# Low parts of half the mixer's weights on GpSimd instead of VectorE

## The chip, the cores and the metric

The kernel runs on one core of a Trainium2 chip. The core has five engines that work side by side, each on its own queue in order: TensorE (PE) multiplies matrices into an accumulator memory (PSUM), VectorE (DVE), ScalarE (ACT) and GpSimd (POOL) work elementwise, SyncE (SP) issues the transfers from the large memory (HBM) into the fast one (SBUF). Semaphores tell one engine that another is done. The metric is the device time of one execution in microseconds, here the median of several runs.

## What is computed

Two layers (`DEPTH`) over 256 tokens of width 1024, each a gated feed-forward, a mixer, a cross attention and a second gated feed-forward, each followed by a normalisation of the sum with the input. The change lies in the mixer:

```python
z = h @ w_in[l]
cb, cc, ch, rq, rf, ri, rg, pu = jnp.split(z, split_at, axis=-1)
y_conv = short_gated_conv(ch, cb, cc, conv_w[l])
y_rec = hgrn2(rq, rf, ri, rg, lbs[l], rec_norm_g[l])
y_pool = multiscale_pool(pu, pool_w[l], pool_scale[l])
mix = jnp.concatenate([y_conv, y_rec, y_pool], axis=-1) @ w_out[l]
h = layer_norm(ALPHA * h + mix, ln_g[l, 1], ln_b[l, 1])
```

`hgrn2` is a gated linear recurrence in chunks of 64 tokens, four heads of 128; the short convolution has three taps; the pool takes sliding means over 2, 4, 8 and 16 tokens. All inputs are float32 and the result has to keep nearly that precision.

## The kernel before

**Two parts for each weight.** TensorE's fast float format keeps fewer bits than float32. So each weight is used as a sum of a high part (the weight rounded to that format) and a low part (what the rounding left), and the activations likewise; a product is high by high, high by low and low by high. `split` (line 58) makes both parts: ScalarE casts the high part (line 59), VectorE subtracts it from the source (line 60). In profiles the weight's parts are `whi` and `wlo`, the loaded weight is `raw`.

**Loading.** `load` (line 62) brings a block of rows and columns of a weight matrix. It takes 128 x 2048 elements at a time into one of three `raw` buffers, with one transfer on SyncE's queue, and splits each in two halves of 128 x 1024 (`s` is 0 or 1, line 77), each with a `whi` and a `wlo` tile of its own from rings of eight. A load of 512 columns over all 1024 rows is two `raw` buffers, so four halves; one of 256 columns is one buffer and two halves; a slab of the output matrix (256 rows, 1024 columns) is also one buffer and two halves. A `whi` or `wlo` tile is written again when TensorE has read its last use, a `raw` buffer when both halves have been cast and subtracted.

**The mixer's order in the program** (function `mixer`, line 518). `columns` (line 522) loads some columns of `w_in` and multiplies: the forget gate f (columns 1280), the query q (768); then v (1792, by its own loop); then the recurrence; the pool's input (2816, 256 columns); the convolution's first two thirds (0) and its last (512, 256 columns); the output gate (2304). `fill` then computes the second half of the attention's keys (`keys(l, 1)`, line 494), and `project_back` multiplies with four slabs of `w_out`.

**The recurrence** is a chain between TensorE and VectorE: two products with the identity (line 576), one product of q with f over 1024 elements (line 579), then seven levels, each with a copy of keys into `kc` (line 585), matmuls (line 591), two products that scale q and k (lines 607 and 608) and two masked copies of the matmuls' results into `AT` (line 610). Two powers on GpSimd (line 640) normalise the result.

**What sets the order.** Each engine runs its instructions in a fixed order, which a planner sets when the program is built, from its own estimates of durations; the program's text gives precedence but not the order itself. So TensorE's matmuls for the pool and the convolution stand interleaved with those of the recurrence. No order is written out by hand around the change. Before it, GpSimd has in the mixer only the powers and some small fills.

Of the kernel before, what the change touches and what calls it, by code (L numbers as in the profile page):

```python
# [8 lines left out]
F32 = mybir.dt.float32  # L9
# [3 lines left out]
ALU = mybir.AluOpType  # L13
# [7 lines left out]
DM = 1024  # L21
DFF = 2816
NT = SEQ // P
NK = DM // P
# [4 lines left out]
CHUNK = 512  # L29
# [17 lines left out]
def model(ctx: ExitStack, tc: tile.TileContext, t: dict, out: bass.AP):  # L47
    nc = tc.nc
# [6 lines left out]
        return ps.tile(list(shape), F32, tag=tag, name=tag)  # L55


    def split(hi, lo, src):
        nc.scalar.copy(hi, src)  # L59
        nc.vector.tensor_tensor(lo, src, hi.bitcast(F32), op=ALU.subtract)  # L60

    def load(src, k0, nk, c0, ncol, fine=False):


        hi, lo, todo = [], [], []
        step = 2048 // ncol
        for a in range(k0, k0 + nk, step):
            raw = wp.tile([P, 2048], F32, tag="raw", name="raw", bufs=3)
            raw = raw.rearrange("p (k c) -> p k c", c=ncol)
            half = step // 2  # L70
            part = 1 if fine else step
            for b in range(0, step, part):
                nc.sync.dma_start(
                    raw[:, b : b + part, :],
                    src[(a + b) * P : (a + b + part) * P, c0 : c0 + ncol].rearrange("(k p) c -> p k c", p=P),
                )
            for s in range(2):
                h = wp.tile([P, 1024], F32R, tag="whi", name="whi", bufs=8)
                w = wp.tile([P, 1024], F32R, tag="wlo", name="wlo", bufs=8)
                h = h.rearrange("p (k c) -> p k c", c=ncol)  # L80
                w = w.rearrange("p (k c) -> p k c", c=ncol)
                r = raw[:, s * half : (s + 1) * half, :]
                if fine:
                    todo += [(h[:, b, :], w[:, b, :], r[:, b, :]) for b in range(half)]
                else:
                    split(h, w, r)
                hi.append(h)
                lo.append(w)
        return Weights(hi, lo, half, todo)
# [20 lines left out]
    def mm_cols(w, cols, x):  # L110
        o = acc()
        for k in range(NK - 1):
            product(o, w.at(k, cols)[0], x[:, k], k == 0, False)
        for k in range(NK):
            product(o[:, 0, :], w.at(k, cols)[1], x[:, k, 0, :], False, False)
        product(o, w.at(NK - 1, cols)[0], x[:, NK - 1], False, True)
        return sums(o)

    def add(dst, o):
        dst = dst if len(dst.shape) == 3 else halves(dst)  # L120
        nc.scalar.copy(dst, o[:, 1])  # L121
        nc.vector.tensor_tensor(dst, o[:, 0], dst, op=ALU.add)  # L122
# [17 lines left out]
    h = [cst.tile([P, DM], F32, name=f"h{i}") for i in range(NT)]  # L140
    for i in range(NT):
        for n in range(2):
            c = slice(n * 512, n * 512 + 512)
# [13 lines left out]
    xTh, xTl = xT[:, :, 0, :], xT[:, :, 1, :]  # L157
# [4 lines left out]
    def transposed(src, i, dh, dl, unit=idn):  # L162
        for j in range(2):
            pt = acc((P, 4, P))
            for k in range(4):
                nc.tensor.transpose(pt[:, k, :], src[:, (4 * j + k) * P : (4 * j + k + 1) * P], unit)  # L166
            split(dh[:, 4 * j : 4 * j + 4, tok(i)], dl[:, 4 * j : 4 * j + 4, tok(i)], pt)
# [89 lines left out]
    def ln_params(l, n):  # L257
        g = wp.tile([P, DM], F32, tag="lng", name="lng")
        b = wp.tile([P, DM], F32, tag="lnb", name="lnb")
        nc.sync.dma_start(g, t["ln_g"][l, n : n + 1, :].to_broadcast([P, DM]))  # L260
        nc.sync.dma_start(b, t["ln_b"][l, n : n + 1, :].to_broadcast([P, DM]))
        return g, b
# [81 lines left out]
    def ffn(l, name, n, pend=None, last=False, early=None):  # L344
        gate, up, down = (t[f"{name}_{x}"][l] for x in ("gate", "up", "down"))
        with tc.tile_pool(name="ffn", bufs=2, reuse_waits="tile") as fp:
# [7 lines left out]
            def first():  # L354

                ah, al = act_tiles()
                wg = load(gate, 0, NK, 0, CHUNK, fine=pend is None)
                wu = load(up, 0, NK, 0, CHUNK) if pend is not None else None

                def products(o, w, i, k):  # L360
# [10 lines left out]
                def turn(i, s):  # L371
                    pt = acc((P, 4, P))
                    for k in range(4):
                        nc.tensor.transpose(pt[:, k, :], s[:, k * P : (k + 1) * P], idn)  # L374
                    split(ah[:, :, tok(i)], al[:, :, tok(i)], pt)

                if pend is None:
# [5 lines left out]
                    with tc.manual_schedule(engines={E.Activation, E.DVE, E.PE}):  # L383
# [5 lines left out]
                        for a in range(0, NK, 2):  # L389
                            for k in range(a + 4, min(a + 6, NK)):  # L390
                                split(*wg.todo[k])
                            group(0, wg, a)
                    wu = load(up, 0, NK, 0, CHUNK)
                    for a in range(0, NK, 2):
                        group(1, wu, a)
# [96 lines left out]


    def keys(l, c, between={}):
        w = load(t["ca_k"][l], 0, NK, c * CHUNK, CHUNK)
        for p in range(2):
            o = sm.tile([P, 2, SEQ], F32, tag="sums", name="sums", bufs=1)
            for j in range(2):
                between.get(4 * p + 2 * j, lambda: None)()
                add(o[:, j, :], mm_cols(w, slice((2 * p + j) * P, (2 * p + j + 1) * P), mT))  # L500
            d = slice(4 * c + 2 * p, 4 * c + 2 * p + 2)
            split(kTh[:, d, :], kTl[:, d, :], o)
# [15 lines left out]
    def mixer(l, fill):  # L518
        w_in = t["w_in"][l]
        with tc.tile_pool(name="mix", bufs=1, reuse_waits="tile") as mp:  # L520

            def columns(c0, ncol, take, behind=lambda p: None):
                w = load(w_in, 0, NK, c0, ncol)
                for j in range(ncol // P):
                    take(j, mm_cols(w, slice(j * P, (j + 1) * P), xT))
                    if j % 2:
                        behind(j // 2)
# [8 lines left out]
            def ev_f(p):  # L536
# [10 lines left out]
                )  # L547

            columns(1280, 512, lambda j, o: add(f[:, :, j, :], o), ev_f)
            columns(768, 512, lambda j, o: add(q[:, :, j, :], o))  # L550
            gb = ln_params(l, 1)
            w = load(w_in, 0, NK, 1792, 512)
            for i in range(NT):
                o = acc((P, 512))
                for kk in range(NK):
# [26 lines left out]
            for n, c in enumerate(LEVELS):  # L582
                a = 64 // c
# [44 lines left out]
            for i in range(NT):  # L628
                o = acc((P, HEADS, P), "dn")
                for hh in range(HEADS):  # L630
                    c = slice(hh * P, hh * P + P)
# [20 lines left out]
            for x in (pu, *pw):  # L652
                nc.gpsimd.memset(x[:, :, 0:PAD], 0.0)

            columns(2816, 256, lambda j, o: add_forward(pu[:, j, PAD:], o))
            win = mp.tile([P, 2, SEQ], F32, name="win")
            src = pu
            for g, w_ in enumerate(WINDOWS):
# [4 lines left out]
                    op=ALU.add,  # L663
# [4 lines left out]
                src = d  # L668
# [45 lines left out]
            fill()  # L714

            def slab(a):
                return lambda: (load(t["w_out"][l], a, 2, 0, DM), xTh[:, a : a + 2, :], xTl[:, a : a + 2, :])

            return project_back([slab(a) for a in (0, 6, 2, 4)], 3, gb, 1.0)


# [86 lines left out]
    for l in range(DEPTH):  # L808
        pend = ffn(l, "ffn1", 0, pend, early=None if l else lambda op: (load_memory(op), small_parameters(op)))
        keys(l, 0, {6: pend})  # L810
        pend = mixer(l, lambda: keys(l, 1))
        pend = attention(l, pend)
        pend = ffn(l, "ffn2", 3, pend, last=l == DEPTH - 1)
# [27 lines left out]
```

## Time and profile before

| what | value |
|---|---|
| time, median of 3 runs | 1120.82 us (1120.36 to 1121.79) |
| time of the profiled execution | 1121.47 us |
| its span, first to last instruction | 1119.8 us |
| TensorE busy | 1105.0 us |
| VectorE busy | 821.2 us |
| ScalarE busy | 592.9 us |
| GpSimd busy | 40.3 us |
| mean granted TensorE clock | 0.999 of full speed |

A row of a group of instructions reads: line of the kernel, engine, operation, written tile `<-` read tiles, shapes and types, count, then busy time in us and mean ns of one, and the engine's idle time ahead of them with what ended it. A row of the timeline reads: start and duration in us, engine, line, operation, tiles, count; in brackets the idle time before and who ended it. A duration in the timeline of several merged instructions runs from the first start to the last end. A row of a wait reads: engine, line and tile, `<-` who was waited for, total us, times, longest. Rows by stretch give the length, then for each engine busy us and instructions, the granted clock, the share of the transfer engines and GB/s. TensorE's busy time is a model of pipelined matmuls, so a full TensorE row means that it had matmuls queued throughout. PEld stands for TensorE's weight loads.

### The profile page before, as it was taken

The page shows a single profiled execution, that of the slowest core. Times are in us where ns is not written, and L with a number is a line of the kernel's source. Part 1 is how long each engine was busy: PE and PEld are TensorE (multiplying, and loading weights), DVE is VectorE, ACT ScalarE, POOL GpSimd, SP SyncE. Part 2 cuts the span into 40 slices and gives each one's busy share as a digit, 9 for nine tenths or more (in the row PEclk, how much of TensorE's full clock was granted, in tenths as well). Part 3 has the DMA queues.
Part 4 walks back from the last instruction along what each step waited for, and adds up shares of the span by engine and source line. Part 5 has one row for each costly group of instructions (what it writes and reads, how often), then busy time and mean ns, then how long its engine had stood idle before and what let it go on. Part 6 is the DMA issues. An engine that isn't in the chain of part 4 may idle for free.

```text
span 1119.8 us, 15741 instructions
## 1 busy us (share of the span) xinstructions
PE 1105.0 (99%) x6219; PEld 991.1 (89%) x6219; DVE 821.2 (73%) x1194; ACT 592.9 (53%) x873; POOL 40.3 (4%) x80
## 2 busy tenths in 40 slices
PE   8999999999999999999999999999999999999997
PEld 6989988989889889999889999889888898999996
DVE  5766668889888676666677665697998777766665
ACT  6665553625466456555365555456354663655550
POOL 7000000000000000000000000000000000000000
PEclk9999999999999999999999999999999999999999
DMA  9756564743565375656466655756155644755551
GB/s 338 268 193 218 179 237 147 234 146 127 212 229 185 110 248 206 226 193 210 161 225 226 213 180 188 239 184 217 60 218 175 245 151 154 255 192 201 181 183 38
DMA packets 98522, 218.23 MB, mean 195 GB/s; under 512 B 3792, under 2 KB 16368, under 8 KB 98448
## 3 DMA queue, kind: packets, MB, share of 16 engines
q1 hardware_dynamic: 97968, 216.68, 56.1%
q8 instruction: 49, 0.80, 0.3%
q10 hardware_dynamic: 288, 0.39, 0.1%
q14 instruction: 25, 0.20, 0.1%
q0 software_dynamic: 192, 0.15, 0.0%
HBM read 216.15 MB, written 1.05 MB: 194 GB/s over the span
## 4 chain that ended last, share of the span: by engine, by line
PE 90%; DVE 7%; issue 1%; DMA 0%; ACT 0%; SPq 0%; DVEq 0%; ACTq 0%
PE acc L101 60%; PE dn L101 27%; DVE wlo L60 3%; PE acc L166 1%; PE dn L591 1%; DVE xT L60 1%; DVE h L306 1%; DMA raw<-in_ffn_gate_dram 0%; ACT whi L59 0%; DVE AT L610 0%; DVE h L292 0%; DVE h L302 0%; PE dn L634 0%; PE acc L374 0%; DVE st L294 0%
## 5 line engine op out<-in xcount | busy, mean ns | idle before, releaser
L60 DVE TENSOR_TENSOR wlo<-raw,whi 128x1024 fp32r<-128x1024 f32 (+1 forms) x396 | 470.0, 1211 | 111.7 <-ACT whi L59 77.4
L59 ACT CAST whi<-raw 128x1024 fp32r<-128x1024 f32 (+1 forms) x396 | 398.7, 1041 | 189.6 <-PE dn L101 125.1
L101 PE MATMUL acc<-xT,whi 128*128 128x512 f32 x1600 | 389.4, 381 | 0.7 <-DVE xT L60 0.7
L101 PEld LDWEIGHTS acc<-xT,whi 128*128 128x128 f32 x1600 | 288.4, 190 | 33.6 <-DVE xT L60 1.1
L101 PEld LDWEIGHTS acc<-xT,wlo 128*128 128x128 f32 x1600 | 209.8, 191 | 10.6
L101 PE MATMUL acc<-xT,wlo 128*128 128x256 f32 x1600 | 211.3, 275 | 0.0
L101 PE MATMUL dn<-whi,ah 128*128 128x512 f32 x346 | 131.6, 380 | 0.0
L101 PE MATMUL dn<-wlo,ah 128*128 128x512 f32 x346 | 131.1, 379 | 0.0
L101 PE MATMUL dn<-whi,al 128*128 128x512 f32 x346 | 131.1, 379 | 0.0
L101 PE MATMUL acc<-whi,xT 128*128 128x512 f32 x320 | 99.0, 387 | 0.2 <-ACT whi L59 0.2
L122 DVE TENSOR_TENSOR sg<-acc,sg 128x256 f32<-128x256 f32 x72 | 30.4, 422 | 69.4 <-ACT sg L121 69.3
L101 PE MATMUL dn<-whi,xT 128*128 128x512 f32 x256 | 77.8, 380 | 0.0
L101 PEld LDWEIGHTS dn<-whi,al 128*128 128x128 f32 x346 | 65.4, 189 | 9.3
L101 PEld LDWEIGHTS dn<-wlo,ah 128*128 128x128 f32 x346 | 65.4, 189 | 9.1
L101 PEld LDWEIGHTS dn<-whi,ah 128*128 128x128 f32 x346 | 65.5, 189 | 8.6
L121 ACT COPY sg<-acc 128x256 f32<-128x256 f32 x72 | 26.7, 370 | 82.8 <-PE acc L101 82.8
L101 PEld LDWEIGHTS acc<-whi,xT 128*128 128x128 f32 x320 | 61.6, 193 | 9.6 <-ACT whi L59 0.6
L101 PE MATMUL acc<-wlo,xT 128*128 128x512 f32 x160 | 61.8, 386 | 0.0
L101 PEld LDWEIGHTS dn<-whi,xT 128*128 128x128 f32 x256 | 48.2, 189 | 6.6
L121 ACT COPY up<-acc 128x256 f32<-128x256 f32 x72 | 26.7, 371 | 49.3 <-PE acc L101 48.2
L299 POOL TENSOR_TENSOR rs<-rs,nhalf 128x1 f32<-128x1 f32 x16 | 14.9, 933 | 938.6 <-DVE rs L298 938.6
L101 PE MATMUL dn<-wlo,xT 128*128 128x512 f32 x128 | 48.5, 379 | 0.0
(192 smaller groups left out, 1042.9 us busy)
## 6 DMA issues: line engine op xcount, KB each, us to landing
raw<-in_ffn_up_dram SPq DMA_DIRECT2D x44, 1024.0 KB, 5.0
raw<-in_ffn_down_dram SPq DMA_DIRECT2D x44, 1024.0 KB, 4.9
raw<-in_ffn_gate_dram SPq DMA_DIRECT2D x42, 1024.0 KB, 5.0
raw<-in_w_in_dram SPq DMA_DIRECT2D x24, 1024.0 KB, 5.0
raw<-in_ca_k_dram SPq DMA_DIRECT2D x8, 1024.0 KB, 5.0
raw<-in_w_out_dram SPq DMA_DIRECT2D x8, 1024.0 KB, 4.9
raw<-in_ca_v_dram SPq DMA_DIRECT2D x8, 1024.0 KB, 5.7
raw<-in_ca_q_dram SPq DMA_DIRECT2D x8, 1024.0 KB, 4.9
```

What stands on the lines that cost most here:

```text
L59: nc.scalar.copy(hi, src)
L60: nc.vector.tensor_tensor(lo, src, hi.bitcast(F32), op=ALU.subtract)
L101: nc.tensor.matmul(o, w, x, start=start, stop=stop)
L121: nc.scalar.copy(dst, o[:, 1])
L122: nc.vector.tensor_tensor(dst, o[:, 0], dst, op=ALU.add)
L166: nc.tensor.transpose(pt[:, k, :], src[:, (4 * j + k) * P : (4 * j + k + 1) * P], unit)
L299: nc.gpsimd.tensor_tensor(rs, rs, nhalf[:, 0:1], op=ALU.pow)
L306: nc.vector.scalar_tensor_tensor(h[i][:, c], h[i][:, c], rs, b[:, c], op0=ALU.mult, op1=ALU.add)
L591: nc.tensor.matmul(o[:, hh], kc[:, hh, :], view(qf, hh * P + c, (other - c, 2), (2 * c, a), (1, c)), start=True, stop=True,)
```

## The change

`split` gets a parameter `by`, the engine that subtracts, VectorE unless told otherwise. `load` gets a parameter `shared`; where it is set, the second half (`s` = 1) of each `raw` buffer is subtracted by GpSimd. ScalarE's casts stay. `shared` is set for the mixer's loads of `w_in` except that of the forget gate (1280), for the second half of the keys' columns, and for the four slabs of `w_out`, in both layers. The loads of the feed-forwards, of the attention and of the first half of the keys are as before. The arithmetic is the same.

```diff
-    def split(hi, lo, src):
+    def split(hi, lo, src, by=nc.vector):
         nc.scalar.copy(hi, src)
-        nc.vector.tensor_tensor(lo, src, hi.bitcast(F32), op=ALU.subtract)
+        by.tensor_tensor(lo, src, hi.bitcast(F32), op=ALU.subtract)
 
-    def load(src, k0, nk, c0, ncol, fine=False):
+    def load(src, k0, nk, c0, ncol, fine=False, shared=False):
...
-                    split(h, w, r)
+                    split(h, w, r, nc.gpsimd if shared and s else nc.vector)
...
     def keys(l, c, between={}):
-        w = load(t["ca_k"][l], 0, NK, c * CHUNK, CHUNK)
+        w = load(t["ca_k"][l], 0, NK, c * CHUNK, CHUNK, shared=c == 1)
...
             def columns(c0, ncol, take, behind=lambda p: None):
-                w = load(w_in, 0, NK, c0, ncol)
+                w = load(w_in, 0, NK, c0, ncol, shared=c0 != 1280)
...
-            w = load(w_in, 0, NK, 1792, 512)
+            w = load(w_in, 0, NK, 1792, 512, shared=True)
...
             def slab(a):
-                return lambda: (load(t["w_out"][l], a, 2, 0, DM), xTh[:, a : a + 2, :], xTl[:, a : a + 2, :])
+                return lambda: (load(t["w_out"][l], a, 2, 0, DM, shared=True), xTh[:, a : a + 2, :], xTl[:, a : a + 2, :])
```

## The prediction, made before the changed kernel was run

> **What bounds the kernel now.** I read the head of the page first.
>
> ```profile
> span 1119.8 us, 15741 instructions
> PE 1105.0 (99%) x6219; PEld 991.1 (89%) x6219; DVE 821.2 (73%) x1194; ACT 592.9 (53%) x873; POOL 40.3 (4%) x80
> ```
>
> TensorE (PE) is busy 1105.0 of 1119.8 us, so no edit on another engine can win more than the 14.8 us in which it is not, and the change touches only the two mixers. Next the busy times by stage: four stretches of the first mixer (loads of q and v; the recurrent chain; pool, convolution, gate and keys; the output product), then the chain of the second.
>
> ```profile
> core 0: us, PE busy (x) PEld busy (x) DVE busy (x) ACT busy (x) POOL busy (x), PEclk, DMA share, GB/s
> 199.35:230.75 31.40, 31.40 (x177) 28.40 (x178) 24.88 (x38) 20.04 (x28) 0.00 (x0) 1.00 0.72 240
> 230.75:258.66 27.91, 27.32 (x191) 24.35 (x190) 27.68 (x61) 9.02 (x19) 0.00 (x0) 1.00 0.23 76
> 258.66:288.89 30.23, 29.90 (x185) 27.05 (x184) 27.52 (x56) 16.59 (x38) 2.03 (x2) 1.00 0.56 191
> 288.89:302.04 13.15, 13.15 (x62) 11.53 (x61) 9.55 (x11) 6.16 (x9) 0.00 (x0) 1.00 0.77 280
> 780.84:808.80 27.96, 27.34 (x192) 24.36 (x190) 27.73 (x61) 9.01 (x19) 0.00 (x0) 1.00 0.22 76
> ```
>
> VectorE (DVE) is full in the recurrent chain (27.68 of 27.91 us) and nearly full behind it (27.52 of 30.23), GpSimd (POOL) is empty. Yet PE loses only 27.91 - 27.32 = 0.59 us in the chain and 0.33 us behind it, 0.92 us a mixer; the second mixer repeats it (0.62). The waits of PE and of its weight loads around the first mixer say on whom:
>
> ```profile
> PE dn L591 <- DVE kc L585: 0.6, 1, 0.6
> PE acc L101 <- DVE xT L60: 0.3, 2, 0.2
> PE acc L101 <- DVE sums L122: 0.2, 1, 0.2
> PEld dn L591 <- issue: 1.4, 3, 1.0
> PEld acc L101 <- DVE xT L60: 0.6, 1, 0.6
> ```
>
> So PE bounds the kernel, and in the chain VectorE runs in step with it, with no slack: the matmuls of the levels (line 591) start as VectorE delivers.
>
> **What the change removes.** The groups by shape of that stretch, and three subtracts back to back elsewhere, give the price on VectorE.
>
> ```profile
> L60 DVE TENSOR_TENSOR wlo<-raw,whi 128x1024 fp32r<-128x1024 f32 x34 | 40.8, 1223 | 5.1 <-ACT whi L59 5.0
> 33.16 3.49 DVE L60 TENSOR_TENSOR wlo<-raw,whi 128x1024 fp32r<-128x1024 f32 x3
> ```
>
> One lasts 1.22 us; in a row each further one adds (3.49 - 1.22)/2 = 1.13 us. By the code a 512-column load makes four low parts, two of them second halves; a 256-column load and an output slab make two, one of them a second half. Moved in each mixer: 2 (q) + 2 (v) + 1 (pool) + 2 (convolution) + 1 (its third part) + 2 (gate) + 2 (keys) + 4 (output) = 16, which takes 16 x 1.13 = 18.1 us from VectorE. Off the critical path that is worth nothing; it is worth something where VectorE is late, at most the 0.92 us of PE idle a mixer, and part of the weight-load waits.
>
> **What it adds.** Sixteen two-input subtracts of 1024 elements on GpSimd. The trace has none. The nearest rows are one-input work and powers:
>
> ```profile
> L218 POOL CAST masks<-mf 128x896 uint8<-128x896 f32 x1 | 0.9, 926 | 0.1
> L151 POOL TENSOR_SCALAR_AFFINE_SELECT jdn<-jdn 128x128 f32<-128x128 f32 x1 | 0.3, 297 | 0.0
> L299 POOL TENSOR_TENSOR rs<-rs,nhalf 128x1 f32<-128x1 f32 x16 | 14.9, 933 | 938.6 <-DVE rs L298 938.6
> L640 POOL TENSOR_TENSOR ss<-ss,nhalf 128x4 f32<-128x4 f32 x4 | 4.1, 1016 | 135.2 <-DVE ss L639 135.2
> ```
>
> From below: the cast, 0.926 us for 896 elements, gives 1.06 us for 1024 with one input. From above: four powers take 83 ns more than one, 28 ns an element, 28 us for 1024; 16 of these would be far more than the mixer lasts. That row is a power and not a subtraction, so I value near the cast: two inputs at the cast's rate one after the other, 2.1 us, with 0.1 us to start 2.2 us. I keep 4.4 us as the upper case. [...]
>
> **Whether the two engines hinder each other.** This decides, and the start of the trace shows it, where GpSimd builds masks beside VectorE's subtracts.
>
> ```profile
> 19.88 0.24 POOL L210 TENSOR_SCALAR_AFFINE_SELECT mf<-mf 128x64 f32<-128x64 f32 x1
> 16.62 1.23 DVE L60 TENSOR_TENSOR wlo<-raw,whi 128x1024 fp32r<-128x1024 f32 x1 [1.75 <-ACT whi L59]
> 17.96 1.18 POOL L210 TENSOR_SCALAR_AFFINE_SELECT mf<-mf 128x64 f32<-128x64 f32 x1
> 17.77 1.26 DVE L60 TENSOR_TENSOR wlo<-raw,whi 128x1024 fp32r<-128x1024 f32 x1
> ```
>
> The same select takes 0.24 us alone and 1.18 us beside a subtract, ending as the subtract does: GpSimd stood still for a whole VectorE instruction. The other direction shows small here: the subtracts start 17.77 - 16.62 = 1.15 us apart in place of 1.13, but a select reads only 64 elements. Bounds for what a GpSimd subtract costs a VectorE instruction that wants to start: 0.02 us below (that row), 2.2 us above (its whole length). I take the upper end, since the select waited for whole instructions, and put the lower end into the rivals. [...]
>
> **Where it strikes.** ScalarE's casts set when a second half is ready for GpSimd; these are the ones that fall around the chain (second halves of the convolution's load, its third part and the gate), with VectorE's and PE's rows.
>
> ```profile
> 228.41 1.05 ACT L59 CAST whi<-raw 128x1024 fp32r<-128x1024 f32 x1 [0.26 <-PE acc L101]
> 231.43 1.05 ACT L59 CAST whi<-raw 128x1024 fp32r<-128x1024 f32 x1
> 240.55 1.05 ACT L59 CAST whi<-raw 128x1024 fp32r<-128x1024 f32 x1
> 228.19 3.82 DVE L60 TENSOR_TENSOR wlo<-raw,whi 128x1024 fp32r<-128x1024 f32 x3 [3.46 <-ACT whi L59]
> 231.93 0.68 DVE L576 TENSOR_TENSOR AT<-dn,idn 128x512 f32<-128x512 f32 x1
> 232.53 1.22 DVE L60 TENSOR_TENSOR wlo<-raw,whi 128x1024 fp32r<-128x1024 f32 x1
> 234.26 1.22 DVE L579 TENSOR_TENSOR q<-q,f 128x1024 f32<-128x1024 f32 x1
> 241.60 0.70 DVE L608 TENSOR_TENSOR k<-k,tot 128x512 f32<-128x512 f32 x1
> 242.40 0.42 DVE L585 COPY kc<-k 128x512 f32<-128x512 f32 x1
> 235.53 1.18 PE L591 MATMUL dn<-q,kc 128*128 128x128 f32 x8
> 241.66 1.13 PE L591 MATMUL dn<-q,kc 128*128 128x128 f32 x8 [0.59 <-DVE kc L585]
> ```
>
> First, GpSimd's subtract of the half cast at 228.41 runs from 229.5 to 231.7. VectorE's remaining subtract, wanted at 230.8, ends at 232.8; the two products with the identity follow until 234.0 (one input in PSUM each, so not held up). The half cast at 231.43 goes to GpSimd from 232.8 to 235.0, and the product of line 579, which could start at 234.0, starts at 235.0 in place of 234.3: the chain is 0.8 us late, although two subtracts left VectorE in front of it. Second, the gate's half is cast by about 242.4 with that delay. GpSimd gets its turn behind the product of line 608 (then 242.4 to 243.0) and holds until 245.2; the 0.2 us addition from PSUM passes, the copy of line 585 is wanted at 243.2 and waits 2.0 us. Behind it on VectorE's queue are all later levels, and PE, in order, waits for each. The chain ends 0.8 + 2.0 = 2.8 us late, and PE has nothing to put there, since its columns are already interleaved in a fixed order. Behind the chain VectorE loses six subtracts of the gate, keys and first two slabs (6 x 1.13 = 6.8 us) and meets five GpSimd subtracts, each up to 2.2 us less the PSUM-fed work it can do meanwhile (I take 0.8 us): 5 x 1.4 = 7.0 us. I cost that at nothing. If that cover is gone, the PSUM copies of keys are late, where PE already waits:
>
> ```profile
> 283.55 1.78 PE L101 MATMUL acc<-mT,whi 128*128 128x512 f32 x7 [0.25 <-DVE sums L122]
> ```
>
> Before the chain there is room; v's casts and first product with a low part:
>
> ```profile
> 207.92 2.94 ACT L59 CAST whi<-raw 128x1024 fp32r<-128x1024 f32 x3
> 220.60 0.38 PE L101 MATMUL acc<-wlo,xT 128*128 128x512 f32 x1
> ```
>
> Three halves are cast by 210.9 and the first low part is read at 220.6, ten us on; VectorE's 31.40 - 24.88 = 6.5 us of idle there take what it loses. Buffers of raw weights come free when both halves are read; VectorE's half is the later one in the chain, so transfers on SP's queue move little. GpSimd's own queue holds the two powers of line 640: a subtract put ahead of one makes VectorE's line 641 wait up to 2.2 us more; I count it with the third rival.
>
> **Sum**: 2 x 2.8 = 5.6 us. The profiled execution took 1121.47 us (span 1119.8), so 1127.1 by it; it lies 0.65 us over the median of the runs, 1120.82, so the forecast is **1126.4 us**.
>
> **Rivals.** (1) *Hidden.* GpSimd reads in pieces and VectorE hardly notices (0.02 us a time); the relief lies beside PE, which is fed anyway: 1120.8, give or take 2. For it: PE's 0.92 us of idle. Against: the 1.18 us select. (2) *Faster.* With no hold-up the chain starts up to 2 x 1.13 = 2.3 us sooner, before line 579; the level matmuls then find their operands and PE's idle goes, 2 x 0.92 = 1.8 us, and some of the weight-load waits, 1.4 us in the first mixer (2.8 in both): 1119.0 to 1116.2, I say 1118. It decides as soon as a GpSimd subtract costs VectorE less than the 1.13 us that it saves. (3) *VectorE becomes the bound.* Each of the 16 costs 2.2 - 1.13 = 1.07 us net, 17.1 us a mixer; from 199.35 to 288.89 VectorE has 6.5 + 0.2 + 2.7 = 9.4 us of idle to take it; 7.7 us are left, twice: 1136.2. Against: several fall before the chain where VectorE is idle. (4) *The low part itself is late.* The last slab's second half is tightest:
>
> ```profile
> 291.28 1.06 ACT L59 CAST whi<-raw 128x1024 fp32r<-128x1024 f32 x1
> 297.52 0.38 PE L101 MATMUL dn<-wlo,xT 128*128 128x512 f32 x1
> ```
>
> Cast by 292.3 and used at 297.5, it has 5.2 us. At 2.2 us, even behind another, it is in time; at 4.4 us behind one that started at 290.1 it ends at 298.9, 1.4 us late, twice: 1123.6.
>
> **Chances.** Forecast 0.44, hidden 0.25, faster 0.14, VectorE bound 0.12, late low part 0.05. About 0.2% (2.2 us) can be told from no change. Slower: 0.44 + 0.12 + 0.05 = 0.61; same: the hidden case and 0.04 of the faster one (its 1119.0 end), 0.29; faster: 0.10. The likeliest alone spans 1123.5 (only the 2.0 us of the gate's half, once) to 1130 (0.8 + 2.0 + one power held up 2.2 us, 5.0 a mixer, less its overlap). The range reaches into the faster case and to the bound of the third: 1118.3 to 1136.2; what it leaves out is the 28 us price, which I give no weight, the far end of the faster case and what lies beyond the third.
>
> **What will show it.** GpSimd's group of 32 subtracts near 2.2 us or longer (1.2 would speak for the lower bound). VectorE's instructions at lines 579, 585, 607 and 608 that overlap one of them: lengthened by 1 to 2 us if they are held up, unchanged at 1.2 and 0.4 to 0.9 us if not. PE's idle in the two chain stretches: about 3.4 us each if I am right, below 0.6 if the change is a gain. The first matmuls of the output product 2.8 us later than 288.89. Wrong would be a chain stretch as long as before with GpSimd active in it, or a loss that sits behind the chain alone. The order of instructions is fixed anew when the program is built; if it puts the subtracts elsewhere, the places shift and the price of a meeting is what is left of this.

## The result and the profile after

The changed kernel takes 1139.61 us (median of 5 runs, 1138.25 to 1142.88) against 1120.82 us before: ratio 1.0175, 95% interval 1.0164 to 1.0186, so 18.8 us or 1.7% slower. The direction was forecast, the size is more than three times the forecast 5.6 us and lies outside the range. The profiled execution took 1139.24 us, its span is 1137.5 us, 17.7 us more than before.

The head of the page and the groups by line; line numbers are one higher than before behind line 62.

```profile
span 1137.5 us, 15790 instructions
PE 1106.8 (97%) x6219; PEld 993.3 (87%) x6219; DVE 834.0 (73%) x1162; ACT 592.8 (52%) x873; POOL 131.0 (12%) x112
L60 DVE TENSOR_TENSOR wlo<-raw,whi 128x1024 fp32r<-128x1024 f32 (+1 forms) x364 | 455.9, 1274 | 111.7 <-ACT whi L59 75.5
L60 POOL TENSOR_TENSOR wlo<-raw,whi 128x1024 fp32r<-128x1024 f32 x32 | 89.0, 2793 | 95.7 <-ACT whi L59 95.7
```

VectorE has 32 subtracts fewer and is busier, 834.0 us against 821.2: its busy time counts the time in which an instruction stands still (the product of line 609 below has 2.78 us, where its like had 0.70). The first mixer by the same four stages (its recurrent chain starts at 229.19, its output product at 297.02; columns as in the prediction):

```profile
197.80:229.19 31.39, 31.39 (x177) 28.42 (x178) 26.74 (x31) 19.59 (x28) 19.30 (x7) 1.00 0.69 225
229.19:258.91 29.72, 25.73 (x183) 23.45 (x182) 29.51 (x57) 6.83 (x18) 6.18 (x3) 1.00 0.24 85
258.91:297.02 38.11, 33.62 (x193) 29.68 (x192) 30.68 (x54) 20.67 (x41) 15.30 (x7) 0.96 0.49 166
297.02:310.20 13.18, 13.18 (x63) 11.56 (x62) 9.31 (x9) 4.68 (x7) 6.06 (x2) 1.00 0.72 231
```

PE idles 29.72 - 25.73 = 3.99 us in the chain (0.59 before) and 38.11 - 33.62 = 4.49 us behind it (0.33 before), where its granted clock also falls to a mean of 0.96. VectorE is full in the chain, but behind it has 7.4 us of idle: it is not short of time there. PE's waits in the whole execution, each two or four times, that is, in both mixers:

```profile
PE acc L102 <- DVE yr L713: 4.6, 2, 2.3
PE dn L592 <- DVE q L608: 4.2, 4, 1.9
PE acc L102 <- DVE sg L649: 3.5, 2, 1.7
PE dn L592 <- DVE q L580: 3.4, 2, 1.7
```

Four pairs in the timeline show what lies behind each of the four, GpSimd's subtract and the VectorE instruction that met it:

```profile
231.00 2.66 POOL L60 TENSOR_TENSOR wlo<-raw,whi 128x1024 fp32r<-128x1024 f32 x1 [0.65 <-ACT whi L59]
232.55 2.19 DVE L580 TENSOR_TENSOR q<-q,f 128x1024 f32<-128x1024 f32 x1
243.09 2.36 POOL L60 TENSOR_TENSOR wlo<-raw,whi 128x1024 fp32r<-128x1024 f32 x1 [9.44 <-ACT whi L59]
243.22 2.78 DVE L609 TENSOR_TENSOR k<-k,tot 128x512 f32<-128x512 f32 x1
281.30 2.46 POOL L60 TENSOR_TENSOR wlo<-raw,whi 128x1024 fp32r<-128x1024 f32 x1 [7.95 <-ACT whi L59]
281.78 2.54 DVE L60 TENSOR_TENSOR xT<-cv,xT 128x512 fp32r<-128x512 f32 x1 [0.24 <-ACT xT L59]
286.39 2.35 POOL L60 TENSOR_TENSOR wlo<-raw,whi 128x1024 fp32r<-128x1024 f32 x1 [2.63 <-ACT whi L59]
286.37 2.78 DVE L701 TENSOR_SCALAR sg<-sg,prm 128x256 f32<-128x256 f32 x2
```

The product of line 609 lasts 2.78 us, where its like took 0.70 before; it ends at 246.00, 0.55 us after GpSimd's subtract (243.09 + 2.36 = 245.45). The gate's two scalings of line 701 take 2.78 us together; that is an instruction with one tensor input in SBUF and one scalar a row. PE, at the other end (the last column in brackets is its idle time and who ended it):

```profile
234.79 1.18 PE L592 MATMUL dn<-q,kc 128*128 128x128 f32 x8 [1.70 <-DVE q L580]
247.19 1.16 PE L592 MATMUL dn<-q,kc 128*128 128x128 f32 x8 [1.93 <-DVE q L608]
284.86 1.75 PE L102 MATMUL acc<-mT,whi 128*128 128x512 f32 x7 [1.73 <-DVE sg L649]
290.00 3.12 PE L102 MATMUL acc<-mT,whi 128*128 128x512 f32 x7 [2.28 <-DVE yr L713]
292.92 1.43 PE L102 MATMUL acc<-mT,wlo 128*128 128x256 f32 x8
```

The two waits of 1.73 and 2.28 us are for accumulators: the gate's last columns and the transposed recurrence sit in PSUM until VectorE has read them, behind the two instructions that stood still, and the keys' matmuls need their places. Behind the last wait seven matmuls take 3.12 us in place of 1.75, and the next eight 1.43 in place of 1.05. The granted clock shows why. In these traces it changes only at whole steps of 3.413 us, counted from its first rise (here at 6.97 us); three such steps around the last wait (the column behind GpSimd's is the granted clock):

```profile
286.87:290.28 3.41, 1.13 (x8) 0.83 (x7) 3.31 (x4) 0.30 (x1) 1.87 (x1) 1.00 0.56 148
290.28:293.69 3.41, 3.41 (x11) 2.81 (x11) 2.73 (x6) 1.81 (x4) 0.00 (x0) 0.50 0.77 297
293.69:297.11 3.42, 3.42 (x24) 3.18 (x23) 1.24 (x3) 2.45 (x4) 0.01 (x1) 1.00 0.02 5
```

In the first step PE is idle for 3.41 - 1.13 = 2.28 us; the whole next step runs at 0.50, and the third at 1.00 again. The second mixer repeats it.

So a mixer loses 3.99 - 0.59 = 3.4 us in the chain, 4.49 - 0.33 = 4.2 us behind it, and 3.41 x 0.50 = 1.7 us to the slower clock: 9.3 us. By the rows, the two stretches last 29.72 + 38.11 = 67.83 us against 27.91 + 30.23 = 58.14, which is 9.7 us more, and the second mixer's 67.83 us against 58.18. The span grew by less than twice that, 17.7 us, because in this execution the first chain starts 1.56 us earlier (229.19 against 230.75). That start varies from execution to execution: over all the traces it lies between 228.28 and 231.81 us, the later, in the main, the later the clock first rises (6.97 to 15.54 us).

### The profile page after: what moved, and what is told of

Its sections match the earlier page's. It is cut to its first block, busy times and chain, and to the rows that moved or that the text cites. A ratio compares the mean times of both kernels' runs of the same rounds, so it can differ in the third digit from the quotient of the medians.

```text
span 1137.5 us, 15790 instructions
## 1 busy us (share of the span) xinstructions
PE 1106.8 (97%) x6219; PEld 993.3 (87%) x6219; DVE 834.0 (73%) x1162; ACT 592.8 (52%) x873; POOL 131.0 (12%) x112
## 3 DMA queue, kind: packets, MB, share of 16 engines
HBM read 216.15 MB, written 1.05 MB: 191 GB/s over the span
## 4 chain that ended last, share of the span: by engine, by line
PE 84%; DVE 10%; issue 2%; ACT 2%; DMA 2%; SPq 0%; DVEq 0%; ACTq 0%
PE acc L102 55%; PE dn L102 27%; DVE wlo L60 3%; ACT whi L59 1%; DMA raw<-in_ffn_up_dram 1%; PE acc L167 1%; DVE k L609 1%; DVE xT L60 1%; PE dn L592 1%; DVE h L307 1%; DVE sg L701 0%; DMA raw<-in_ffn_gate_dram 0%; DVE q L608 0%; DVE AT L611 0%; DVE q L580 0%
## 5 line engine op out<-in xcount | busy, mean ns | idle before, releaser
L60 DVE TENSOR_TENSOR wlo<-raw,whi 128x1024 fp32r<-128x1024 f32 (+1 forms) x364 | 455.9, 1274 | 111.7 <-ACT whi L59 75.5
L60 POOL TENSOR_TENSOR wlo<-raw,whi 128x1024 fp32r<-128x1024 f32 x32 | 89.0, 2793 | 95.7 <-ACT whi L59 95.7
```

The source lines that it names most:

```text
L60: by.tensor_tensor(lo, src, hi.bitcast(F32), op=ALU.subtract)
```

## The experiments

Theory *collisions*: while GpSimd reads from SBUF, VectorE's instructions that have all their inputs there stand still (and the reverse), and the cost depends on what stands still. Rivals: *new order*, the planner's other order costs the time; *late low parts*, GpSimd's results come too late for PE. Each experiment was timed against the kernel before on the same chip.

**The change in three places, one at a time.** Nothing but the loads with `shared` differs from the changed kernel.

Ahead of the chain, the loads of q and v:

```diff
-        w = load(t["ca_k"][l], 0, NK, c * CHUNK, CHUNK, shared=c == 1)
+        w = load(t["ca_k"][l], 0, NK, c * CHUNK, CHUNK, shared=False)
-                w = load(w_in, 0, NK, c0, ncol, shared=c0 != 1280)
+                w = load(w_in, 0, NK, c0, ncol, shared=c0 in (768, ))
...
-                return lambda: (load(t["w_out"][l], a, 2, 0, DM, shared=True), xTh[:, a : a + 2, :], xTl[:, a : a + 2, :])
+                return lambda: (load(t["w_out"][l], a, 2, 0, DM, shared=False), xTh[:, a : a + 2, :], xTl[:, a : a + 2, :])
```

> GpSimd subtracts only the second halves of the loads of q and v, four a mixer, ahead of the recurrent chain. Theory 'collisions' (VectorE stands still while GpSimd reads, and what counts is where it stands still): VectorE had 6.5 us idle in that stretch, so 1120.8, within 2 us, although VectorE's subtracts there lengthen to 2 to 3 us. Rival 'new order' (what costs is the order that the planner makes of the changed program, not the port): any share of the change brings a good part of the 18.8 us, 1125 or more. Rival 'late low parts' (PE waits for what GpSimd makes too slowly): 1121, its halves are ready early.

Measured: 1120.30 us against 1120.70, ratio 0.9997 (0.9987 to 1.0006): no difference. Yet the engines collide there as much as anywhere; from its timeline:

```profile
200.15 6.49 POOL L60 TENSOR_TENSOR wlo<-raw,whi 128x1024 fp32r<-128x1024 f32 x2 [6.50 <-ACT whi L59]
199.87 4.53 DVE L60 TENSOR_TENSOR wlo<-raw,whi 128x1024 fp32r<-128x1024 f32 x2
```

Two VectorE subtracts take 4.53 us in place of 2.36, two of GpSimd 6.49. Nobody waits for them.

Around the chain, the loads of the pool, the convolution and the gate:

```diff
-                w = load(w_in, 0, NK, c0, ncol, shared=c0 != 1280)
+                w = load(w_in, 0, NK, c0, ncol, shared=c0 in (2816, 0, 512, 2304, ))
...
```

> GpSimd subtracts only the second halves of the pool's, convolution's and gate's loads, six a mixer; keys and output slabs back on VectorE. 'Collisions': the loss of PE in the chain stays (measured 3.4 us a mixer above before), the one behind it goes: 1120.8 + 6.8 = 1127.6, between 1125 and 1130, and PE's granted clock stays 1.00 throughout. 'New order': not told apart from it by the time alone. 'Late low parts': PE would wait on a low part of GpSimd, and it does not in the changed kernel, so 1121.

Measured: 1129.33 us (1125.35 to 1129.81), ratio 1.0069 (1.0050 to 1.0089), 8.6 us slower. PE's waits of the chain are those of the changed kernel (1.7 us for line 580 and 1.9 us for line 608, in each mixer), and those behind it are gone. I had expected the clock at 1.00 throughout, and it was not. These are the clock's steps around the longer wait, two of the first mixer and two of the second:

```profile
246.36:249.78 3.42, 1.49 (x14) 1.30 (x13) 3.42 (x7) 0.00 (x0) 0.87 (x1) 1.00 0.00 0
249.78:253.19 3.41, 3.41 (x13) 2.87 (x12) 3.22 (x8) 0.37 (x1) 0.00 (x0) 0.50 0.01 2
799.32:802.74 3.42, 2.64 (x18) 2.02 (x17) 3.42 (x5) 0.84 (x2) 2.36 (x1) 1.00 0.02 5
802.74:806.15 3.41, 2.18 (x15) 2.08 (x16) 3.41 (x10) 0.00 (x0) 0.00 (x0) 1.00 0.00 0
```

The wait is 1.93 us in both mixers. In the first it lies within one step (3.42 - 1.49 = 1.93 us of idle), and the next step runs at 0.50. In the second the end of a step, at 802.74, cuts it into two, and the clock stays at 1.00. 2 x 3.4 + 1.7 = 8.5 us.

Behind the chain, the keys and the output slabs:

```diff
-                w = load(w_in, 0, NK, c0, ncol, shared=c0 != 1280)
+                w = load(w_in, 0, NK, c0, ncol, shared=c0 in ())
-            w = load(w_in, 0, NK, 1792, 512, shared=True)
+            w = load(w_in, 0, NK, 1792, 512, shared=False)
...
```

> GpSimd subtracts only in the keys' load and the four output slabs, six a mixer. 'Collisions': the loss behind the chain stays: 4.2 us of PE idle and 1.7 us of slow clock a mixer, 1120.8 + 11.8 = 1132.6, between 1129 and 1135, with the clock near 0.57 for some 3.5 us after PE's idle. The chain stretch as before. 'Late low parts': PE waits at the output product, not at the keys.

Measured: 1132.83 us, ratio 1.0108 (1.0093 to 1.0123), 12.1 us slower; PE waits 4.5 us for line 713 and 4.5 us for line 649 over both mixers, and only 0.2 us for a low part, one of VectorE's. The three parts add up to -0.4 + 8.6 + 12.1 = 20.3 us against 18.8 for the whole.

The output slabs alone (the keys' load back on VectorE too):

> GpSimd subtracts only in the four output slabs, four a mixer. 'Collisions': in the changed kernel the two instructions on the path to PE that stood still behind the chain (the split of the convolution's result, 2.54 us, and the gate's scaling, 2.78 us) stood behind subtracts of output slabs, so nearly the whole loss of the run with keys and slabs stays: 1129 to 1133. If the keys' two subtracts carry half of it: 1126 to 1127.

Measured: 1128.45 us, ratio 1.0066 (1.0050 to 1.0083), 7.75 us slower, between the two ranges that I had expected. The gate's scaling still stands still:

```profile
283.17 2.54 POOL L60 TENSOR_TENSOR wlo<-raw,whi 128x1024 fp32r<-128x1024 f32 x1 [3.76 <-ACT whi L59]
283.15 2.71 DVE L701 TENSOR_SCALAR sg<-sg,prm 128x256 f32<-128x256 f32 x2
```

So two of three parts of this loss are the output slabs' and 12.1 - 7.75 = 4.4 us come with the keys'. The slabs' subtracts run here although their results are wanted only some 10 us later.

**Is it GpSimd's reading?** Two kernels with the same order of instructions on VectorE, PE and ScalarE. VectorE makes all low parts again; ahead of each of the 32 that the change moves, GpSimd writes into the same tile, zeros in one kernel, a copy of the loaded half in the other, and VectorE's subtract waits for that.

```diff
-                    split(h, w, r, nc.gpsimd if shared and s else nc.vector)
+                    nc.scalar.copy(h, r)
+                    if shared and s:
+                        nc.gpsimd.memset(w.bitcast(F32), 0.0)
+                    nc.vector.tensor_tensor(w, r, h.bitcast(F32), op=ALU.subtract)
```

In the second kernel the line of the fill is `nc.gpsimd.tensor_copy(w, r)`.

> VectorE makes all low parts again; ahead of each of the 16 moved subtracts a mixer GpSimd fills the same tile with zeros (it writes and reads nothing), and VectorE's subtract waits for it. 'Collisions at GpSimd's reads': VectorE's instructions keep their lengths beside a fill; the time is 1120.8 plus what the new waits cost, 1120 to 1124. 'Every use of the memory by GpSimd stops VectorE': as the run with the copy. 'New order': 1125 or more.

> The same program with the same order on every engine, but GpSimd copies the loaded half into the tile in place of the zeros: one input read, near 1.1 us each. 'Collisions at GpSimd's reads': VectorE's two-input instructions beside a copy lengthen by up to 1 us, 16 times a mixer, and nothing has left VectorE's queue: 4 to 16 us over the run with the fills. 'New order' and 'late low parts': equal to the run with the fills, since order and waits are the same.

Measured: with the fills 1121.48 us, ratio 1.0005 (0.9995 to 1.0014), no difference; with the copies 1129.99 us, ratio 1.0081 (1.0066 to 1.0096), 8.5 us over the fills. The low parts' instructions by tile, in the kernel with copies (count, then minimum, median and maximum in ns):

```profile
L90 DVE TENSOR_TENSOR wlo<-raw,whi x388: 1170/1218/2092, 17.0 to 1100.8; 128x1024 fp32r<-128x1024 f32 x194
L89 POOL CAST wlo<-raw x32: 1036/1052/2039, 197.1 to 847.1; 128x1024 fp32r<-128x1024 f32 x32
```

And in the kernel with fills:

```profile
L90 DVE TENSOR_TENSOR wlo<-raw,whi x388: 1172/1219/1259, 17.0 to 1094.8; 128x1024 fp32r<-128x1024 f32 x194
L89 POOL MEMSET wlo<- x32: 948/952/959, 199.4 to 841.0; 128x1024 f32 x32
```

A fill takes 0.95 us and a copy 1.04 us alone, nearly the same. Beside fills no VectorE subtract passes 1259 ns and no fill passes 959; beside copies they reach 2092 and 2039, nearly a length of the other added, in both directions. In the two traces TensorE, VectorE and ScalarE run the same instructions in the same order, and the copy waits for nothing that VectorE's subtract does not wait for too, so it is the reading.

**What is the relief worth without a collision?** GpSimd writes zeros twice (1.9 us, near its subtract's length) and nobody makes these low parts; this leaves the low parts of the second halves out.

```diff
-                    split(h, w, r, nc.gpsimd if shared and s else nc.vector)
+                    nc.scalar.copy(h, r)
+                    if shared and s:
+                        for _ in range(2):
+                            nc.gpsimd.memset(w.bitcast(F32), 0.0)
+                    else:
+                        nc.vector.tensor_tensor(w, r, h.bitcast(F32), op=ALU.subtract)
```

> VectorE is relieved of the 16 subtracts a mixer as in the change, but GpSimd writes zeros twice in their place and reads nothing; so this leaves out the low parts of these halves, and shows what the relief is worth without a collision. 'Collisions': no VectorE instruction stands still, PE's waits in the mixers go or shrink, 1118 to 1120.8. 'New order' (the planner sees nearly the same program as the changed one): 1125 or more.

Measured: 1118.17 us, ratio 0.9979 (0.9969 to 0.9989), 2.4 us faster. PE's waits in the mixers for the keys' copies and sums, 1.7 us in both mixers before, are gone; 0.3 us remain for line 608. So the relief by itself is a gain. This run also answers *new order*: its matmuls stand in the changed kernel's order without exception, and all but 28 of VectorE's 1162 instructions do, so that order costs nothing. And the two runs with the output slabs, which lose 7.75 and 12.1 us, have the matmul order of the kernel before.

**Shorter stops.** The change with each GpSimd subtract in two instructions of 512 elements:

```diff
+                    n = 1 if not (shared and s) else 2
+                    for z in range(n):
+                        d = slice(z * ncol // n, (z + 1) * ncol // n)
+                        (nc.gpsimd if shared and s else nc.vector).tensor_tensor(
+                            w[:, :, d], r[:, :, d], h[:, :, d].bitcast(F32), op=ALU.subtract
+                        )
```

> The change with each GpSimd subtract cut in two of 512 elements. 'Collisions': a stop is half as long (near 1.2 us), but there are twice as many and VectorE's instruction in between can pass; the sum of the blocked time stays much the same where VectorE is busy, so 1134 to 1140, with no VectorE instruction over 2.6 us. If the length of one stop decides (PE's slack of a microsecond hides a short one): 1128 or less.

Measured: 1138.81 us, ratio 1.0162 (1.0147 to 1.0177), as the change. GpSimd's 64 instructions sum to 105.4 us (89.0 for the 32 whole ones). By the changed kernel's line numbers, the product of line 609 lasts 1.71 us in place of 2.78, but others meet both halves: the product of line 580 lasts 2.32 us, the two scalings of the gate 2.62 us. VectorE's busy time falls to 821.1 us (834.0 with whole ones), but PE still waits 2.8 us for line 713 and 2.0 us for line 580 in each mixer.

**Is the slow clock PE's idle?** The changed kernel with matmuls whose results nobody uses, where PE waits:

```diff
+                if c == 1 and (p, j) in ((0, 1), (1, 0)):
+                    d = acc(tag="dn")
+                    for _ in range(8 if j else 10):
+                        product(d, w.at(0, slice(0, P))[0], mT[:, 0], True, True)
                 add(o[:, j, :], mm_cols(w, slice((2 * p + j) * P, (2 * p + j + 1) * P), mT))
```

> The changed kernel with 8 and 10 more matmuls (128 x 512, 0.216 us each, results not used) in the keys' load of each mixer, where PE waits 1.73 and 2.28 us; they run in PE's idle and add little. 'The clock drops because PE stood idle': the granted clock stays 1.00 behind them, the time falls by up to 2 x 1.7 us: 1136 to 1138. 'The clock drops for another reason': it drops as before, 1139.6 or more.

Measured: the median is 1138.57 us, but of four runs between 1136.58 and 1143.77, so the time decides nothing. The profile does, at the place in question: PE is busy there and the clock stays.

```profile
282.00:288.00 6.00, 5.98 (x34) 5.10 (x34) 6.00 (x6) 2.85 (x5) 3.38 (x2) 1.00 0.48 175
288.00:294.00 6.00, 5.87 (x32) 4.96 (x31) 4.72 (x10) 2.68 (x6) 0.29 (x1) 1.00 0.57 178
804.00:814.00 10.00, 9.18 (x52) 8.36 (x53) 8.36 (x21) 0.37 (x1) 0.00 (x0) 0.83 0.00 0
```

The second mixer's tail is the same, at 1.00. The last row is the chain of the second mixer, which was not filled: there the clock fell this time, where it had not in the changed kernel; the wait of 1.93 us lay within one of its steps (802.32 to 805.74). The profiled execution took 1137.1 us against 1139.24.

**Relief bought elsewhere.** Two versions of the kernel before use ScalarE in place of GpSimd: for the copies of keys in the chain, and for the scalings of lines 667 and 700.

```diff
-                nc.vector.tensor_copy(
+                nc.scalar.copy(
                     kc.rearrange("p h (a w c) -> p w (h a) c", w=2, c=c),
```

> The kernel before, with the copies of keys (line 585) on ScalarE, which is idle for 19 of the 27.9 us of the chain stretch; GpSimd has no part in it. It asks if relief of VectorE in the chain is worth anything where it is bought without GpSimd: seven copies of some 0.4 us a mixer. If VectorE alone sets the chain, PE's 0.59 us of idle goes: 1119 to 1120.5. If the way over a third engine costs as much as it saves: 1121 to 1124.

Measured: 1121.96 us, ratio 1.0012 (1.0002 to 1.0021), no gain: the second case that I had expected.

```diff
-                nc.vector.tensor_scalar_mul(win[pr, j, PAD:], d[pr, j, 2 * PAD :], 1.0 / w_)
+                nc.scalar.mul(win[pr, j, PAD:], d[pr, j, 2 * PAD :], 1.0 / w_)
...
-                    nc.vector.tensor_scalar_mul(sg[:, hh, :], sg[:, hh, :], ng[:, l, hh : hh + 1])
+                    nc.scalar.mul(sg[:, hh, :], sg[:, hh, :], ng[:, l, hh : hh + 1])
```

> The kernel before, with VectorE relieved without GpSimd: the gate's scaling (line 700) and the sliding means' scaling (line 667) move to ScalarE, four instructions of 0.36 and four of 0.27 us a mixer. If any relief of VectorE in the mixer comes out as less PE idle, as in the run with the zeros (16 subtracts less: 2.4 us): 1119.5 to 1120.5. If only relief at the places where PE waits counts, or ScalarE's slower instructions on the gate's path cost as much: 1120.6 to 1122.

Measured: 1122.79 us, ratio 1.0020 (1.0011 to 1.0029): slower. PE now waits 1.1 us a mixer for line 712, behind the gate's scaling on ScalarE. That is above both ranges. In both versions, the moved instruction itself stands on the way to PE, and the relief gained nothing; that the one is the reason for the other was not tested. No version that computes everything was faster than the kernel before.

## Why the prediction was right in kind and wrong in size

**What bounds the kernel, and the ceiling of a gain: right.** The relief without collisions gave 2.4 us; the prediction had 1.8 us of PE idle plus a part of the weight-load waits, 1118 us for its second rival (between 1116.2 and 1119.0), and 1118.17 was measured.

**GpSimd's price: nearly right.** 2.2 us forecast, 2.35 us at the least; the mean of 2.79 us holds GpSimd's own stops behind VectorE. It is nowhere late for PE, so the fourth rival falls; no run shows the 4.4 us of the upper case, the longest subtract of the changed kernel took 3.37 us.

**That a meeting costs the whole instruction: right.** Line 609 rose from 0.70 to 2.78 us; the first rival (0.02 us a meeting) falls with the pair of fills and copies. In that pair, no VectorE subtract passed 1259 ns beside fills, which only write, and one took 2092 ns beside copies, which read. As I had assumed, instructions with an input in PSUM were not held up: the two products with the identity took 0.68 and 0.67 us from 231.35 on, beside GpSimd's subtract, and 0.68 each before. Line 701, with one tensor input in SBUF and one scalar a row, was held up too (2.78 us for two in place of 0.62). That a copy, line 585, would be held up I had assumed without a row for it; in the run with halves it was (1.28 us at 246.57, in place of 0.42).

**The chain: right.** Forecast 2.8 us a mixer, measured 3.4, at the places named: the product of line 579 (580 now, 2.18 us in place of 1.22) and a level behind the gate's half. There the product of line 608 (609 now) stopped for 2.1 us and not the copy behind it, since GpSimd began just ahead of it (243.09 against 243.22). Against the forecast 5.6 us for both mixers stand 6.8.

**The step that failed is this one: behind the chain, "6.8 us" of relief against "7.0 us" of stops, "I cost that at nothing".** Measured there: 4.2 us of PE idle and 1.7 us of slow clock a mixer, 5.9 us, more than the chain. The sum of the stops was right: five VectorE instructions are longer than their like before, by 1.36, 0.23, 1.38, 1.84 and 2.15 us, 7.0 us in all; VectorE even had 7.4 us to spare. But a sum over a queue says nothing about which instruction stands still. Relief fell on subtracts whose results had time, the stops on the split of the convolution and the scaling of the gate, one behind the other on the way by which PSUM is emptied for PE. The prediction named the wait that would then show (the keys' matmuls behind VectorE's reads of PSUM) and quoted its 0.25 us, but gave it no price. With 5.9 + 3.4 = 9.3 us a mixer the time would have been 1139.4. (A slip without weight: the 1123.5 of the likeliest case is counted from the profiled execution; from the median, as the forecast is, it is 1122.8.)

**The slow clock was no term at all.** The profile of before had none (mean 0.999), since PE never idled by microseconds in a mixer (0.62 us at most in a stretch). With PE's idle filled the clock stayed at 1.00 at that place; so there it is a consequence of the waits and not a cause beside them. When it falls can be read from the traces, step by step. Behind every step of 3.41 us with 2.20 to 2.29 us of PE idle (seven of them, in four kernels: the changed one, the two with the output slabs, the one with halves) the next one ran at 0.50 (in the run with halves, the next two); behind none with 1.91 us or less it did. Between, 1.93 us brought it down twice (in the run around the chain and in the one with filled waits), and 1.95 us did not. So the 1.93 us wait of the chain, which the changed kernel and two others have, is decided by chance: it counted in both cases where it lay within one step, and in the changed kernel a step's end cuts it in both mixers. A step need not be idle throughout: 1.93 of its 3.41 us were enough there.

**The third rival, VectorE as the bound**, came nearest by its number (1136.2) and is wrong as a mechanism: behind the chain VectorE has more idle time than before.

**Open.** The 20.3 us of the parts against 18.8 is explained only in part. In the profiled executions the parts have three falls of the clock (one around the chain, two behind it) and the whole has two; a fall costs 1.7 us. But each median is taken over executions that may have more or fewer.

## What to carry to other kernels

An engine that is idle is not free if its work makes the one you relieve stand still, as GpSimd's reads did here (a product of 0.70 us took 2.78): ask which instruction of the busy engine stands still during each moved one, and who waits for that, place by place. A balance over the whole queue hides it; the same 4 moved instructions cost nothing ahead of the chain and 7.75 us for both mixers behind it. On a TensorE-bound kernel look at the clock too when you price a wait of some two microseconds: here waits of 1.93 and 2.28 us cost 1.7 us more where they lay within one of the clock's steps.

## What was not expected of the hardware

An instruction with one SBUF input and one scalar a row (128 x 256, in place) is stopped by GpSimd's subtract just as a two-input one is: 2.78 us for two in place of 0.62. Cutting GpSimd's instruction in two only shifts the stops: VectorE's busy time is 12.9 us less, GpSimd's subtracts take 16.4 us more, and the time is the same. And in these traces TensorE's granted clock changes in steps of 3.41 us: in the changed kernel, behind a step with 2.28 us of PE idle, in one gap, the whole next step runs at 0.50.
